# Dilated attention items with joined visits: two PSUM banks taken in turn by transpositions and value products, in place of one bank for each

## The chip, the cores and the metric

The kernel runs on one core of one Trainium2 chip, in one launch. The metric is the device time of that launch in microseconds (us). A core has five engines that follow their own instruction streams and meet through semaphores: TensorE (PE: matrix products and transpositions; the loading of its weights is shown as PEld), VectorE (DVE), ScalarE (ACT), GpSimd (POOL) and SyncE (SP), which here issues the DMAs. Matrix products land in PSUM, which has eight banks of 128 partitions by 512 floats; ACT and DVE read them from there.

## What is computed

One layer of an encoder block on x (1 x 1024 x 1024, float32) with three attention branches. The change lies in the first, the dilated window attention, of 24 heads of 64 in three groups of eight (window and dilation 128/1, 512/4, 2048/16). Cut to its core, the reference does this for one group:

```python
# positions regrouped by residue class mod dilation; then a band of blocks
sc = jnp.einsum('znqhd,znkhd->znhqk', qb, kw).astype(jnp.float32) * (dh ** -0.5)
sc = jnp.where(valid[None, :, None], sc, NEG_INF)
m = jnp.max(sc, axis=-1, keepdims=True)
p = jnp.exp(sc - m)
l = jnp.sum(p, axis=-1, keepdims=True)
o = jnp.einsum('znhqk,znkhd->znqhd', (p / l).astype(v.dtype), vw)
lse = (m + jnp.log(l))[..., 0]
```

The three groups' outputs are then weighted by a softmax over their `lse`, gated, projected, and merged with the other two branches (grouped-query attention; cross-attention into a memory of 256), followed by an output projection and a norm.

## The kernel before

The kernel goes through stages: norm and projections of the memory branch, the grouped-query branch, the dilated items (here about 600 to 1135 us), the merge, the output projection. In every stage but the last, PE's own order is written out by hand in the code. The two interleaved streams are:

- **Dense units.** A unit is one 128-column slice of the input projection: two halves of 24 products each (`dense`, lines 143, 145, 147: two-part weights `wh`, `wl` by two-part activations `hh`, `hl`) into a bank `d`, of which there are two, taken in turn. After each half, DVE reads `d` (rotary product into `t1a`, `t2a`, lines 830 and 831; or the values, line 862), and POOL adds the rotary parts.
- **Pieces of the dilated items.** An item is one pair of heads in one of the three groups, so there are twelve. `plan` writes out its pieces in a fixed order, over eight query tiles T:
  - `scores` (line 918): query by key into banks `s1`, four tiles at a time, at the end of the item before and at T = 3.
  - `soft` (lines 930 to 938): DVE adds the mask and takes the row minimum of the negated scores; ACT takes exponentials into `pra`, two or four instructions per tile.
  - `trans` (lines 955, 964): PE transposes the probabilities of a tile into a `tr` bank, in two to four blocks, and ACT copies it to `app` (line 967). It runs two tiles behind `soft`, so those of tiles 6 and 7 fall into the next item.
  - `values` (line 895): value blocks are transposed into `tr` at T = 4, 5, 6, and copied by ACT to `avs` (line 897).
  - `pv` (line 981): value products of four tiles into a bank `ov`, and ACT copies it to `og` (line 989). The first four tiles come at T = 7, the other four at T = 3 of the next item. Each is joined into one visit with the `scores` of other tiles, which follow it directly on PE.
  - `stats` (line 1000): the row statistics are transposed into `tr` and copied by ACT to `sr` (lines 1003 to 1007), once for each item, at T = 2 of the next.

`weave` lets the two streams take turns on PE by costs that are given in the code (216 for a dense product, 109 for a transposed block, and so on). The other engines' instructions follow from these through a scheduler with priorities.

Banks come from small helpers. `phase_psum` opens the pool of a stage with the number of banks of each kind; `pss1` hands out the next `s1` bank, `pst` the next `tr` bank (128 x 4 x 128), `pso` the next `ov` bank (128 x 512). With one bank of a kind, a new tile's first write waits until the reader of the last tile is done; with two, it waits for the reader of the tile before that one. Six banks are given out to the stage's pool, two go to `d`.

Of the kernel before, what the change touches and what calls it, by code (L numbers as in the profile page):

```python
# [50 lines left out]
def block(ctx: ExitStack, tc: tile.TileContext, x, xT, memT, cst, msk, bcst, tabA, gpost,  # L51
# [15 lines left out]
    def phase_psum(name, s2=0, s1=0, t=0, o=0):  # L67
        assert 2 * s2 + s1 + t + o <= 6
        bank["n"] = (s2, s1, t, o)
        bank["pool"] = tc.tile_pool(name=name, bufs=1, space=bass.MemoryType.PSUM, reuse_waits="tile")  # L70
        bank["p"] = bank["pool"].__enter__()

    def end_psum():
        bank["pool"].__exit__(None, None, None)
# [4 lines left out]
    def pss1():  # L79
        return bank["p"].tile([P, 512], F32, name="s1", tag="s1", bufs=bank["n"][1])  # L80

    def pst():
        return bank["p"].tile([P, 4, 128], F32, name="tr", tag="t", bufs=bank["n"][2])

    def pso():
        return bank["p"].tile([P, 512], F32, name="ov", tag="o", bufs=bank["n"][3])
# [356 lines left out]
    for k in range(8):  # L443
        if k % 2 == 0:
            load_wkv(k // 2)
        for e in range(2 if k == 0 else 1):
            t = slice(e * 512, e * 512 + 512) if k == 0 else slice(0, S)
# [29 lines left out]
    for c in range(2):  # L477
        t = st.tile([P, 4, 256], F32, name=f"mt{c}", tag=f"xk{c}")
# [311 lines left out]
    close(qp)  # L790
    close(kvp)
    end_psum()
    phase_psum("ps_a", s1=4, t=1, o=1)
    pss1()


# [1 line left out]
    with tc.tile_pool(name="aa", bufs=1, reuse_waits="tile") as aa:  # L798
# [75 lines left out]
        def item(p_, g):  # L874
# [95 lines left out]
            def pv(b):  # L970
                if b == 0:
                    d["og"] = OG[p_, g] = cb.tile([P, S], F32, name="og", bufs=4)
                og, vs = d["og"], d["vs"]
                ov = pso()
                for j in range(4):
                    terms = st.pop(4 * b + j)
                    n = len(terms[0])
                    for i in range(n):
                        for h in range(2):
                            x, z, pp = terms[h][i]  # L980
                            PE.matmul(ov[h * 64:h * 64 + 64, j * 128:j * 128 + 128], vs[:, x, z], pp,  # L981
                                      start=i == 0, stop=i == n - 1)
                if g == 0:
                    dst, src = og[:, b * 512:b * 512 + 512], ov
                else:
                    r = DIL[g] // 2
                    dst = og.rearrange("p (u r) -> p r u", r=DIL[g])[:, b * r:b * r + r]
                    src = ov.rearrange("p (r u) -> p r u", r=r)
                A.activation(dst, src, AF.Copy)

            def stats():
# [35 lines left out]
                soft=[(lambda T=T: soft(T), 300.0) for T in range(NT)],  # L1027
                trans=[(lambda T=T: trans(T), 109.0 * {128: 2, 192: 3, 256: 4}[size[T]]) for T in range(NT)],
                pv=[(lambda b=b: pv(b), 250.0 + sum(213.0 * len(blocks_of(T)) for T in range(4 * b, 4 * b + 4))) for b in range(2)],
                stats=(stats, 109.0))  # L1030

# [118 lines left out]
    with tc.tile_pool(name="mg", bufs=1, reuse_waits="tile") as mg:  # L1150
# [102 lines left out]
        for k in range(8):  # L1253
            raw = wp.tile([P, 1024], F32, name="wr", bufs=WR)
            nc.sync.dma_start(raw, wout[k])
            a = hp.tile([P, D], R, name=f"woh{k}", tag="big")
            b = hp.tile([P, D], R, name=f"wol{k}", tag="big")
            split(a, b, raw)
            wo.append((a, b))
        for T in range(NT):  # L1260
            t = slice(T * 128, T * 128 + 128)
# [166 lines left out]
```

## Time and profile before

| | us |
|---|---|
| runs (three) | 1513.45, 1517.66, 1513.59; median 1513.59 |
| profiled execution, own time | 1517.45 |
| profiled execution, span from first to last instruction | 1515.7 |
| granted TensorE clock over the span (1 is full) | 0.995 |
| dilated items, from the first scores to the last value products | about 602 to 1132 |

The profile is one execution. Rows of the timeline give the start, the length, the engine, the line of the kernel, the operation, output and inputs by the program's names, and the idle time before it with what ended it. A matmul's row is longer than its distance to the next one, since matmuls are pipelined and the profiler models their ends. A row with x3 stands for three such instructions in a run. A line of waits reads: engine, output and line that waited, what it waited for, total us, times, longest.

### The profile page before, as it was taken

Reading aid. Unit: us, or ns where it says so; the run is one execution under the profiler, and the core shown is the slowest. Engines: PE = TensorE matmul, PEld = TensorE weight load, DVE = VectorE, ACT = ScalarE, POOL = GpSimd, SP = SyncE. Lnnn points to the kernel's source line nnn. Section 1 sums busy time; section 2 is a strip of 40 time slices with the busy share of each in tenths; the row PEclk is TensorE's granted clock in tenths of the full one; section 3 lists DMA queues with packets and bytes.
Section 4 is the critical chain, followed back from the end, with each engine's and each line's share of the span. In section 5 each row is a group of like instructions: output and inputs, shape, how many; then the busy total and the mean of one; then the engine's idle time right before and its main releaser. Section 6 shows DMA issues by size and latency. Waiting matters only on the chain.

```text
span 1515.7 us, 20621 instructions
## 1 busy us (share of the span) xinstructions
PE 1479.0 (98%) x7844; PEld 1185.4 (78%) x7844; DVE 838.9 (55%) x1514; ACT 578.3 (38%) x1307; POOL 443.8 (29%) x357
## 2 busy tenths in 40 slices
PE   7999989999999999999999999999999999999998
PEld 7899977666776668888777787877777888888787
DVE  7755567566555426655566567556525432525843
ACT  6533444445444431444434444443443112212321
POOL 1426314444444443321232233123200000223322
PEclk9999999999999999999999999999999999999999
DMA  6332011111121122110221131112126541623432
GB/s 236 104 98 71 29 58 51 63 55 43 60 63 56 42 71 90 42 29 29 62 67 43 43 85 36 38 45 71 56 86 189 171 113 42 209 66 116 127 109 98
DMA packets 55042, 119.77 MB, mean 79 GB/s; under 512 B 13792, under 2 KB 23712, under 8 KB 54816
## 3 DMA queue, kind: packets, MB, share of 16 engines
q1 hardware_dynamic: 54800, 118.34, 24.8%
q8 instruction: 61, 1.00, 0.3%
q14 instruction: 37, 0.30, 0.1%
q10 hardware_dynamic: 144, 0.13, 0.0%
HBM read 96.06 MB, written 22.38 MB: 78 GB/s over the span
## 4 chain that ended last, share of the span: by engine, by line
PE 84%; DVE 7%; ACT 3%; issue 2%; DMA 2%; POOL 1%; SPq 0%; POOLq 0%; DVEq 0%; ACTq 0%
PE d L143 14%; PE d L147 14%; PE d L145 14%; PE sc L125 7%; PE ov L720 4%; PE sc L1282 4%; PE sc L147 3%; PE sc L145 3%; PE sc L143 3%; PE ov L981 2%; PE s L705 2%; PE s L918 2%; PE s L704 2%; PE tr L686 2%; PE d L533 2%
## 5 line engine op out<-in xcount | busy, mean ns | idle before, releaser
L143 PE MATMUL d<-hh,wh 128*128 128x512 f32 x992 | 396.0, 399 | 1.7 <-DVE fth L222 1.7
L147 PE MATMUL d<-hh,wl 128*128 128x512 f32 x992 | 397.4, 401 | 0.0
L145 PE MATMUL d<-hl,wh 128*128 128x512 f32 x992 | 393.4, 397 | 0.0
L105 ACT ACTIVATE wh<-wr 128x1024 fp32r<-128x1024 f32 (+1 forms) x100 | 95.4, 955 | 353.2 <-PE d L145 162.5
L143 PEld LDWEIGHTS d<-hh,wh 128*128 128x128 f32 x992 | 187.2, 189 | 44.9 <-issue 5.0
L145 PEld LDWEIGHTS d<-hl,wh 128*128 128x128 f32 x992 | 187.0, 188 | 42.8 <-issue 5.7
L147 PEld LDWEIGHTS d<-hh,wl 128*128 128x128 f32 x992 | 186.9, 188 | 41.6 <-issue 4.7
L711 POOL TENSOR_TENSOR bl<-bl,bp 128x512 f32<-128x512 f32 x96 | 128.8, 1341 | 141.9 <-ACT bp L707 137.3
L106 DVE TENSOR_TENSOR wl<-wr,wh 128x1024 fp32r<-128x1024 f32 (+1 forms) x100 | 113.9, 1139 | 24.3 <-ACT wh L105 24.1
L687 DVE TENSOR_REDUCE bn<-tr 128x1 f32<-128x512 f32 x128 | 87.6, 689 | 63.6 <-PE tr L686 62.3
L707 ACT ACTIVATE bp<-s 128x512 f32<-128x512 f32 x128 | 75.3, 595 | 84.7 <-PE s L705 84.4
L837 POOL TENSOR_TENSOR aq<-t1a,t2a 128x512 f32<-128x512 f32 x24 | 54.6, 2276 | 173.6 <-DVE t1a L831 167.4
L1183 POOL TENSOR_TENSOR acc<-acc,th 128x1024 f32<-128x1024 f32 x16 | 44.6, 2793 | 204.1 <-DVE th L1182 204.1
L831 DVE SCALAR_TENSOR_TENSOR t2a<-d,tab 32x512 f32<-32x512 f32 x96 | 66.0, 687 | 69.1 <-PE d L147 63.7
L147 PE MATMUL sc<-hh,wl 128*128 128x512 f32 x224 | 87.9, 392 | 2.4 <-DVE wl L106 2.4
L837 POOL TENSOR_TENSOR ak<-t1a,t2a 128x512 f32<-128x512 f32 x24 | 54.6, 2276 | 119.9 <-DVE t1a L830 119.9
L145 PE MATMUL sc<-hl,wh 128*128 128x512 f32 x224 | 87.9, 392 | 0.0
L143 PE MATMUL sc<-hh,wh 128*128 128x512 f32 x224 | 87.9, 392 | 0.0
L830 DVE TENSOR_TENSOR t2a<-d,tab 32x512 f32<-32x512 f32 x96 | 66.0, 687 | 25.1 <-PE d L147 23.9
L930 DVE CUSTOM_DVE_ANT_0 pra<-s,mask 128x192 f32<-128x192 f32 (+2 forms) x192 | 56.8, 349 | 36.2 <-PE s L918 24.4
L967 ACT ACTIVATE app<-tr 128x384 f32<-128x384 f32 (+2 forms) x96 | 45.9, 478 | 80.5 <-PE tr L964 46.3
L125 PE MATMUL sc<-gh,wh 128*128 128x512 f32 x192 | 74.7, 389 | 0.0
(263 smaller groups left out, 2745.7 us busy)
## 6 DMA issues: line engine op xcount, KB each, us to landing
wr<-in_wu SPq DMA_DIRECT2D x76, 512.0 KB
g2d<-fth SPq DMA_DIRECT2D x24, 256.0 KB
wgt<-wgd SPq DMA_DIRECT2D x24, 256.0 KB
ot<-od SPq DMA_DIRECT2D x12, 512.0 KB
gt<-g2d SPq DMA_DIRECT2D x12, 512.0 KB
wr<-in_wbr SPq DMA_DIRECT2D x24, 256.0 KB
thd<-fth SPq DMA_DIRECT2D x20, 256.0 KB
th<-thd SPq DMA_DIRECT2D x10, 512.0 KB
```

The source lines that it names most:

```text
L105: A.activation(dst_h, src, AF.Copy)
L106: V.tensor_tensor(dst_l, src, dst_h.bitcast(F32), op=OP.subtract)
L125: PE.matmul(out_ps, a, b, start=i == 0, stop=i == n - 1)
L143: PE.matmul(dst, wh[:, k, :], hh[k][:, t], start=k == 0, stop=False)
L145: PE.matmul(dst, wh[:, k, :], hl[k][:, t], start=False, stop=False)
L147: PE.matmul(dst, wl[:, k, :], hh[k][:, t], start=False, stop=k == 7)
L687: V.tensor_reduce(st[i]["n"][:, j, c:c + 1], s, axis=AX.X, op=OP.min)
L707: A.activation(pp, s, AF.Exp, scale=-1.0)
L711: G.tensor_tensor(lsum[i % 2], lsum[i % 2], pp, op=OP.add)
L830: return V.tensor_tensor(out, x, y, op=OP.mult)
L831: return V.scalar_tensor_tensor(out, x, scale, y, op0=OP.mult, op1=OP.mult)
L837: G.tensor_tensor(half_of(o, half, g), classes(t1, g), classes(t2, g), op=OP.add)
```

## The change

In the dilated stage the pool has two banks of the kind `tr` and none of the kind `ov`; the value products of `pv` take the next `tr` bank, seen as 128 x 512. The number of banks in the pool stays six. So all visits that write these banks (`trans`, `values`, `stats`, `pv`) take the two in turn, in the order of the program.

```diff
@@ -790,7 +790,7 @@
     close(qp)
     close(kvp)
     end_psum()
-    phase_psum("ps_a", s1=4, t=1, o=1)
+    phase_psum("ps_a", s1=4, t=2)
     pss1()
@@ -971,7 +971,7 @@
                 if b == 0:
                     d["og"] = OG[p_, g] = cb.tile([P, S], F32, name="og", bufs=4)
                 og, vs = d["og"], d["vs"]
-                ov = pso()
+                ov = pst().rearrange("p a b -> p (a b)")
                 for j in range(4):
                     terms = st.pop(4 * b + j)
                     n = len(terms[0])
```

## The prediction

> **What bounds the kernel now.** I read the page first (busy time), then the busy times by stage, then who TensorE (PE) waited for in the stretch that the change touches, then that stretch in order of time.
>
> ```profile
> span 1515.7 us, 20621 instructions
> ...
> PE 1479.0 (98%) x7844; PEld 1185.4 (78%) x7844; DVE 838.9 (55%) x1514; ACT 578.3 (38%) x1307; POOL 443.8 (29%) x357
> ```
>
> PE has work for nearly the whole span, and no other engine passes 55%. So time can come only from gaps on PE. The dilated items run from about 600 to 1135 us; their busy time by stretches (first the length, then each engine's busy time, the granted clock behind the engines) is:
>
> ```profile
> core 0: us, PE busy (x) PEld busy (x) DVE busy (x) ACT busy (x) POOL busy (x), PEclk, DMA share, GB/s
> 600.00:1135.00 535.00, 525.28 (x3163) 422.06 (x3162) 308.73 (x724) 225.07 (x673) 134.59 (x79) 1.00 0.18 52
> ...
> 775.00:820.00 45.00, 42.05 (x255) 33.56 (x255) 29.80 (x56) 17.63 (x57) 14.64 (x6) 1.00 0.12 39
> 820.00:865.00 45.00, 45.00 (x279) 36.44 (x276) 24.89 (x71) 19.07 (x58) 8.89 (x8) 1.00 0.15 41
> ```
>
> PE is idle for 9.7 us of this stage, and unevenly: 2.95 us in one stretch of 45 us, nothing in the next. The view of waits, for PE in this stage, names every one of these gaps:
>
> ```profile
> PE tr L955 <- ACT avs L897: 4.8, 6, 0.8
> PE tr L955 <- ACT app L967: 2.3, 3, 0.8
> PE tr L1000 <- ACT app L967: 1.8, 3, 0.6
> PE tr L964 <- ACT app L967: 0.7, 3, 0.2
> ```
>
> Fifteen waits, 9.6 us, all of one kind: a transposition into `tr` waits until ScalarE (ACT) has copied the visit before it out of the only `tr` bank. The value products write `ov`, the other bank, and are in no line. The groups by line say the same: the two kinds of probability transpositions and the statistics carry the idle time (last column).
>
> ```profile
> L964 PE MATMUL tr<-cs,pra 128*128 128x128 f32 x160 | 26.9, 274 | 0.8 <-ACT app L967 0.7
> L955 PE MATMUL tr<-cs,pra 128*128 128x128 f32 x120 | 20.2, 277 | 7.1 <-ACT avs L897 4.8 <-ACT app L967 2.3
> ...
> L1000 PE MATMUL tr<-cs,sts 128*32 128x128 f32 x12 | 3.3, 278 | 1.8 <-ACT app L967 1.8
> ```
>
> **What one stall really costs.** Two places show the pattern; it recurs in each of the later three head pairs. First, the seam between two items; PE and ACT rows in order of time (start, length):
>
> ```profile
> 772.11 0.60 ACT L989 ACTIVATE og<-ov 128x512 f32<-128x512 f32 x1 [1.03 <-PE ov L981]
> ...
> 776.82 0.39 PE L143 MATMUL d<-hh,wh 128*128 128x512 f32 x1
> 777.04 0.40 PE L145 MATMUL d<-hl,wh 128*128 128x512 f32 x1
> 777.57 0.57 ACT L967 ACTIVATE app<-tr 128x512 f32<-128x512 f32 x1
> 778.19 0.55 PE L955 MATMUL tr<-cs,pra 128*128 128x128 f32 x3 [0.75 <-ACT app L967]
> 779.27 0.39 PE L147 MATMUL d<-hh,wl 128*128 128x512 f32 x1
> 779.74 0.47 ACT L967 ACTIVATE app<-tr 128x384 f32<-128x384 f32 x1
> 780.26 0.28 PE L1000 MATMUL tr<-cs,sts 128*32 128x128 f32 x1 [0.60 <-ACT app L967]
> ...
> 781.53 0.39 PE L147 MATMUL d<-hh,wl 128*128 128x512 f32 x1
> 781.77 0.49 PE L955 MATMUL tr<-cs,pra 128*128 128x128 f32 x3
> ```
>
> Unhindered, a dense product starts 0.22 to 0.23 us after the one before (776.82, 777.04), although its row is 0.39 to 0.40 long, since the rows overlap. So a stall is start to start less 0.23: 778.19 - 777.04 - 0.23 = 0.92, where the idle column says 0.75. Each reported gap is really 0.17 longer: 9.6 + 15 x 0.17 = 12.1 us. Stalls of less than 0.17 us are hidden in the overlap altogether or show as no idle time; at 1127.06 below one costs 1127.06 - 1126.65 - 0.23 = 0.18. I count eight such in the stage's timeline, about 1.1 us together. In all PE loses 13.2 us here.
>
> **The change, part by part.** *The order.* As built, every engine has the same instructions in the same order as before. `weave` steers by costs that are not edited, and the ACT copies keep their places. Only waits differ on PE: the first value product of each of 24 visits gets a wait for ACT, and one transposition more has one. No DMA and no queue moves.
>
> *One bank to two for transpositions.* 140 transposition visits and 24 value-product visits now share two banks in turn, so a visit waits for the copy two visits back, not one. At 778.19 that is the value product, copied out at 772.11 + 0.60 = 772.71; PE could have started at 777.27. The whole 0.92 goes. The probabilities that it reads were made an item earlier. The statistics at 780.26 then come 0.92 earlier with their own 0.76 gone (start 778.58) and need the copy that ends at 777.57 + 0.57 = 778.14: free. The transposition at 781.77 would now come 1.68 earlier, at 780.09, and needs the copy that ends at 779.74 + 0.47 = 780.21. If that copy doesn't move (ACT works in order), PE waits 0.12 us for it, and 0.05 us more for the signal (780.21 to 780.26 above): 0.17 us, three times over, so 0.5 us given back. The second place lies inside an item, where value transpositions (copied by L897) alternate with probability transpositions:
>
> ```profile
> 799.63 0.57 ACT L897 ACTIVATE avs<-tr 128x512 f32<-128x512 f32 x1
> 800.26 0.55 PE L955 MATMUL tr<-cs,pra 128*128 128x128 f32 x3 [0.81 <-ACT avs L897]
> 800.84 0.49 ACT L967 ACTIVATE app<-tr 128x384 f32<-128x384 f32 x1 [0.64 <-PE tr L955]
> ...
> 804.42 0.57 ACT L897 ACTIVATE avs<-tr 128x512 f32<-128x512 f32 x1
> 805.04 0.55 PE L955 MATMUL tr<-cs,pra 128*128 128x128 f32 x3 [0.79 <-ACT avs L897]
> ...
> 807.28 0.60 PE L895 MATMUL tr<-cs,vda 128*128 128x128 f32 x4
> ```
>
> Each of the two L955 rows stalls for 0.81 + 0.17 = 0.98 and 0.79 + 0.17 = 0.96. The second needs, two visits back, the copy of 800.84 to 801.33, and PE comes to it at 805.04 - 0.98 - 0.96 = 803.10: free. The value transposition at 807.28 comes 1.94 earlier, at 805.34, and needs the copy that ends at 804.99: free with 0.35 to spare, even if ACT gains nothing.
>
> *The value products' new wait.* Queued behind it on PE are the dense products and the scores of the next block; ACT's copy L989 waits for it. Before, `ov` was free for a whole half item; now the bank is that of the transposition two visits back. The tightest places are at the end of the stage, where the visits crowd:
>
> ```profile
> 1125.57 1.06 ACT L989 ACTIVATE og<-ov 128x512 f32<-128x512 f32 x1
> 1126.65 0.40 PE L143 MATMUL d<-hh,wh 128*128 128x512 f32 x1
> 1127.06 0.44 PE L964 MATMUL tr<-cs,pra 128*128 128x128 f32 x2
> 1127.53 0.39 ACT L967 ACTIVATE app<-tr 128x256 f32<-128x256 f32 x1 [0.53 <-PE tr L964]
> 1131.44 0.77 PE L981 MATMUL ov<-app,avs 128*64 128x128 f32 x10
> ```
>
> The value products at 1131.44 need the copy that ends at 1127.53 + 0.39 = 1127.92: 3.5 us early. The reverse, a transposition that needs a value product's copy, is tightest at 1127.06: PE is there at 1126.88, the copy ended at 1126.63. So the new waits are met before PE comes to them. A wait that is already met shows no price where transpositions carry one now (the one at 781.77 starts 0.24 us after the row of 781.53, as a dense product would), so I take 0 for the 25 new ones. A wait can't gain time, so their bounds are 0 and 25 times the 0.01 us that the view resolves.
>
> *What is late next.* The two `d` banks. With 1.94 us gained by 805.04, the dense product of this row pair would start at 804.19 and needs VectorE's last read of its bank, which ends at 804.03:
>
> ```profile
> 803.34 0.69 DVE L830 TENSOR_TENSOR t1a<-d,tab 128x512 f32<-128x512 f32 x1
> 806.13 0.39 PE L143 MATMUL d<-hh,wh 128*128 128x512 f32 x1
> ```
>
> 0.16 us are left there, in one place of each of three items: it holds narrowly, and each 0.1 us that VectorE slips costs 0.3 us in all.
>
> **The sum.** 13.2 - 0.5 = 12.7 us. What follows the stage starts from PE's last products in it and moves up with them. The profiled execution (span 1515.7, own time 1517.45) becomes 1503.0 and 1504.8. It lies 3.9 above the median of the three runs (1513.59; the others 1513.45 and 1517.66), and no view shows where those 3.9 us are; I take the stage's stalls to be the same in all. **1513.6 - 12.7 = 1500.9 us.** About 0.3% (4.5 us) is what a measurement of this kernel can tell from no change.
>
> **The rivals.** *1. The waits come back one visit later.* If ACT's copies are the real pace (they sit in its queue behind exponentials that wait for VectorE), the second stall of each pair stays: the one at 805.04 (0.96) and that of the statistics (0.76), three times each, 5.2 us; the gain is 7.5, the time 1506.1. For it: the copies at 777.57 and 799.63 come late after their transpositions. Against: the spare times worked out above, 0.35 us and more.
>
> *2. The gain is lost at the next stage.* PE's longest wait behind the items is this:
>
> ```profile
> 1173.64 0.50 PE L147 MATMUL sc<-hh,wl 128*128 128x512 f32 x1 [2.35 <-DVE wl L106]
> ```
>
> If what feeds it is tied to transfers that don't move, it grows by 12.7 us and the time stays 1513.6. Against: the chain of waits leads from it back to the last filler and value products of the items, which move. That the change doesn't remove the bank as the cause of the waits at all would give the same time; but all four wait lines name a copy out of `tr`.
>
> *3. Slower: the granted clock.* After the wait of 1173.64 the clock is low for a while:
>
> ```profile
> 1174.00:1178.00 4.00, 4.00 (x12) 3.16 (x11) 3.35 (x3) 0.00 (x0) 1.21 (x1) 0.57 0.42 131
> ```
>
> That episode costs 4 x (1 - 0.57) = 1.7 us. If taking the banks in turn brought such an episode at each of the 24 value-product visits, it would cost 41 us: 1513.6 - 12.7 + 41 = 1542. It eats the gain from 8 episodes and is slower by 0.3% from 11. Against: the stage runs at 1.00 throughout, with gaps of 0.8 us and `d` banks that already take turns; the change shortens gaps. The Trainium skill, page "TensorE: Matmul & The Clock Gate", section "A second HAM failure mode: psum-queue depth-cycling", tells of a kernel that cycled through PSUM banks each iteration and whose PE idled between groups often enough for its clock to swing. No row of this stage agrees with it: the clock there is 1.00.
>
> **How the numbers follow.** Forecast 0.76; rival 1 0.13; rival 2, or a bank that isn't the cause, 0.06; rival 3 0.05. The first two are faster than 1509.1: 0.89; within 0.3%: 0.06; slower: 0.05. The low end is all 13.2 us and no slow episode at 1174 (1.7): 1498.7. The high end takes in rival 1 with a little more, 1507.0; it also covers the forecast in a run like the slowest of before (1500.9 + 4.1).
>
> **What would show it.** Right: in the profile after, PE's waits in the items keep no line of `tr` for a copy beyond some 0.2 us in three places; the value products have no idle time; the stretch like 775 to 820 is as full as the next; the last value products come at about 1118.7 instead of 1131.44; VectorE's and ACT's busy time are unchanged. Wrong: lines L955 or L1000 with waits of 0.6 us and more (rival 1), a wait at L147 near 1160 of over 10 us (rival 2), a clock under 1.00 between 600 and 1120 us (rival 3), or a new line of `d` waiting for VectorE (the narrow place).

## The result, and the profile after

The changed kernel took 1502.62 us (median of six, 1501.67 to 1505.91), the kernel before 1514.92 us in the six runs beside it (1513.45 to 1517.66). The ratio is 0.9921, 95% interval 0.9907 to 0.9936: 0.8% faster, 12.3 us. In a later comparison it was 0.9906 (0.989 to 0.9922). The forecast was 1500.9 us and 12.7 us.

The page after, its first part:

```profile
span 1500.2 us, 20621 instructions
...
PE 1474.2 (98%) x7844; PEld 1185.7 (79%) x7844; DVE 838.9 (56%) x1514; ACT 576.4 (38%) x1307; POOL 444.7 (30%) x357
```

The instructions are as many as before and the other engines' busy time is the same within 2 us. The share of PE is the same 98%, so the page alone doesn't tell that something was mended; the busy times of the stage do. A row of them gives the stretch and its length, then busy time and number of instructions of PE, PEld, DVE, ACT and POOL, then the granted clock, the DMA share and GB/s. From the first scores to the last value products, before:

```profile
602.47:1131.44 528.97, 519.25 (x3126) 417.32 (x3125) 304.86 (x716) 223.17 (x670) 133.83 (x79) 1.00 0.18 52
```

and after:

```profile
602.33:1118.46 516.13, 515.78 (x3125) 418.85 (x3124) 305.49 (x716) 221.13 (x670) 134.25 (x79) 1.00 0.18 53
```

The stage is 12.84 us shorter (528.97 to 516.13), with PE idle for 0.35 us in place of 9.7. PE, DVE, ACT and POOL run the same instructions in the same order as before. The view of PE's waits has no line left in this stretch. The groups by line, after (last column: idle time before them):

```profile
L981 PE MATMUL tr<-app,avs 128*64 128x128 f32 x640 | 40.2, 276 | 0.0
...
L964 PE MATMUL tr<-cs,pra 128*128 128x128 f32 x160 | 26.6, 272 | 0.0
L955 PE MATMUL tr<-cs,pra 128*128 128x128 f32 x120 | 19.8, 273 | 0.3
```

L955 had 7.1 us, L964 0.8. The value products, which have the new wait, still show none. The second place of the prediction, in order of time after (rows of PE, its weight load PEld, ACT and DVE):

```profile
798.11 0.60 PE L895 MATMUL tr<-cs,vda 128*128 128x128 f32 x4
...
800.25 0.69 DVE L830 TENSOR_TENSOR t1a<-d,tab 128x512 f32<-128x512 f32 x1
800.73 0.40 PE L147 MATMUL d<-hh,wl 128*128 128x512 f32 x1
801.00 0.19 PEld L143 LDWEIGHTS d<-hh,wh 128*128 128x128 f32 x1 [0.31 <-DVE t1a L830]
801.00 0.50 PE L143 MATMUL d<-hh,wh 128*128 128x512 f32 x1
801.33 0.58 ACT L897 ACTIVATE avs<-tr 128x512 f32<-128x512 f32 x1
801.34 0.39 PE L145 MATMUL d<-hl,wh 128*128 128x512 f32 x1
802.26 0.60 PE L895 MATMUL tr<-cs,vda 128*128 128x128 f32 x4
```

ACT's copy at 801.33 is that of the transpositions at 798.11 and still starts 2.6 us after their end (798.71); but PE needs it only at 802.26, and it ends at 801.91. The copy has not become quicker, PE has stopped waiting for it.

The profiles differ by 15.5 us of span, more than the runs' 12.3. Behind the items the wait at L147 is 1.69 us where it was 2.35, and the clock didn't fall after it. The row and the window behind it:

```profile
1160.00 0.50 PE L147 MATMUL sc<-hh,wl 128*128 128x512 f32 x1 [1.69 <-DVE wl L106]
```

```profile
1160.00:1164.00 4.00, 4.00 (x17) 3.30 (x18) 3.15 (x3) 0.00 (x0) 0.96 (x1) 1.00 0.42 131
```

Before, the clock behind this wait (1174 to 1178) stood at 0.57, which cost 1.7 us. These 2.4 us of the two profiles' difference (0.66 and 1.7) vary between executions, as the experiments show; the length of the stage after came out the same when it was profiled again (516.12 us).

### The profile page after: what moved, and what is told of

Its sections match the earlier page's. It is cut to its first block, busy times and chain, and to the rows that moved or that the text cites. A ratio compares the mean times of both kernels' runs of the same rounds, so it can differ in the third digit from the quotient of the medians.

```text
span 1500.2 us, 20621 instructions
## 1 busy us (share of the span) xinstructions
PE 1474.2 (98%) x7844; PEld 1185.7 (79%) x7844; DVE 838.9 (56%) x1514; ACT 576.4 (38%) x1307; POOL 444.7 (30%) x357
## 4 chain that ended last, share of the span: by engine, by line
PE 88%; DVE 5%; DMA 2%; ACT 2%; issue 2%; POOL 1%; SPq 0%; POOLq 0%; DVEq 0%; ACTq 0%
PE d L143 14%; PE d L147 14%; PE d L145 14%; PE sc L125 7%; PE ov L720 4%; PE sc L1282 4%; PE sc L147 3%; PE sc L143 3%; PE sc L145 3%; PE tr L981 3%; PE s L918 2%; PE s L705 2%; PE s L704 2%; PE tr L686 2%; PE d L533 2%
## 5 line engine op out<-in xcount | busy, mean ns | idle before, releaser
L143 PE MATMUL d<-hh,wh 128*128 128x512 f32 x992 | 396.4, 400 | 1.8 <-DVE fth L222 1.8
L147 PE MATMUL d<-hh,wl 128*128 128x512 f32 x992 | 397.4, 401 | 0.0
L143 PEld LDWEIGHTS d<-hh,wh 128*128 128x128 f32 x992 | 187.1, 189 | 47.1 <-issue 5.0
L147 PEld LDWEIGHTS d<-hh,wl 128*128 128x128 f32 x992 | 187.0, 188 | 42.1 <-issue 4.7
L147 PE MATMUL sc<-hh,wl 128*128 128x512 f32 x224 | 87.3, 390 | 1.7 <-DVE wl L106 1.7
L143 PE MATMUL sc<-hh,wh 128*128 128x512 f32 x224 | 87.3, 390 | 0.0
L125 PE MATMUL sc<-gl,wh 128*128 128x512 f32 x192 | 74.7, 389 | 0.0
```

What stands on the lines that cost most here:

```text
L125: PE.matmul(out_ps, a, b, start=i == 0, stop=i == n - 1)
L143: PE.matmul(dst, wh[:, k, :], hh[k][:, t], start=k == 0, stop=False)
L147: PE.matmul(dst, wl[:, k, :], hh[k][:, t], start=False, stop=k == 7)
```

## The experiments

Times are compared with the kernel before on the same chip: 1516.2 us (1512.6 to 1519.16) for the first four, 1517.45 us (1514.07 to 1519.2) for the last two.

### One bank for all: is it the sharing or the second bank?

```diff
-    phase_psum("ps_a", s1=4, t=2)
+    phase_psum("ps_a", s1=4, t=1)
```

> The changed kernel with one tr bank instead of two, so that transpositions and value products share a single bank and the sixth bank of the pool lies idle. My theory (what counts is that a visit waits for the copy two visits back, not that the value products moved): all the waits of before return, 13.1 us as before plus at most some 0.5 us where a transposition now waits for a value product's copy at the end of the stage; 1515 us (1513 to 1518), and the PE waits on tr are again L955, L1000 and L964 with about 9.6 us together, none of them at L981. Rival (the gain came from the value products sharing the bank, or from the changed placement of the program): the time stays at 1502 to 1504.

Measured: 1516.04 us, ratio 1.0004 (0.9994 to 1.0014). PE's waits around this stage:

```profile
PE tr L955 <- ACT avs L897: 4.8, 6, 0.8
PE sc L147 <- DVE wl L106: 2.4, 1, 2.4
PE tr L955 <- ACT app L967: 2.3, 3, 0.8
PE tr L1000 <- ACT app L967: 1.8, 3, 0.6
PE tr L964 <- ACT app L967: 0.7, 3, 0.2
PE tr L964 <- ACT og L989: 0.3, 1, 0.3
```

All four lines of before are back with the same sums. Only one is new, 0.3 us for a value product's copy, at the crowded end. The stage:

```profile
602.00:1131.43 529.43, 519.42 (x3125) 417.19 (x3124) 304.87 (x716) 223.22 (x670) 133.79 (x79) 1.00 0.17 52
```

So seven banks do nearly what eight did before: `ov` as a bank of its own was worth 0.46 us of the stage (529.43 less 528.97; the idle column shows 0.3 of it), and the same bank as a second `tr` is worth 13.30 us (529.43 less 516.13). The Trainium skill, page "Perfetto Trace Analysis", section "Matmul Optimizations", advises to use all eight banks. Here that alone isn't enough: the kernel before used eight and was as slow as this one with seven.

### Two `tr` banks and an `ov` bank, with one score bank less

```diff
-    phase_psum("ps_a", s1=4, t=1, o=1)
+    phase_psum("ps_a", s1=3, t=2, o=1)
```

> The kernel of before with two tr banks and one ov bank, taken from the scores, which get three banks instead of four. My theory: the waits on tr go as in the change, but each of the 24 score visits writes four banks at once, and the fourth now waits until VectorE has read the first for two tiles: in the trace of before, the third of those reads ends some 1.9 us after the visit's start, while PE would be there after 0.75 us, so some 1.1 us each, 27 us in all; 1502.6 + 27 = 1530 us (1520 to 1545), with L918 as a new line of PE's waits. Rival (any two banks for the transpositions do, whoever gives one up): 1502 to 1504, and no line L918.

Measured: 1527.58 us, ratio 1.008 (1.0065 to 1.0096). The waits on `tr` are gone here too. The group of the scores, the first visit, and the part of the second one that waited longest:

```profile
L918 PE MATMUL s<-ak,aq 64*128 64x192 f32 (+2 forms) x384 | 51.8, 349 | 12.7 <-DVE sts L930 12.7
```

```profile
602.70 1.45 PE L918 MATMUL s<-ak,aq 64*128 64x192 f32 x10
604.52 1.13 PE L918 MATMUL s<-ak,aq 64*128 64x256 f32 x6 [0.37 <-DVE sts L930]
605.58 0.50 PE L147 MATMUL d<-hh,wl 128*128 128x512 f32 x1
...
618.90 1.86 PE L918 MATMUL s<-ak,aq 64*128 64x256 f32 x6 [1.63 <-DVE sts L930]
```

The first visit takes 605.58 - 602.70 = 2.88 us; before, such a visit took 1.82. Over the 24 visits I add up 62.8 us against 35.3: 27.5 us, of which the idle column shows 12.7. The wait of 1.63 us was also followed by a stretch of low clock, in which its visit took 4.97 us:

```profile
620.00:630.00 10.00, 10.00 (x40) 7.84 (x39) 4.18 (x12) 4.09 (x15) 0.00 (x0) 0.71 0.07 26
```

The kernel gains the 13 us and pays twice that. The low clock is in the profiled run (1529.63 us at a mean clock of 0.994); the three others took 1527.40 to 1527.73 us at 0.997. Where the bank comes from decides.

### The copies twice, with one bank and with two

In each of the two kernels, the copies of probabilities and of values out of `tr` are done twice in a row:

```diff
                 A.activation(vs[:, i0:i0 + n].rearrange("p b h d -> p b (h d)"), tp[:, :n], AF.Copy)
+                A.activation(vs[:, i0:i0 + n].rearrange("p b h d -> p b (h d)"), tp[:, :n], AF.Copy)
...
                 A.activation(pp[:, :k], tp[:, :k], AF.Copy)
+                A.activation(pp[:, :k], tp[:, :k], AF.Copy)
```

> The kernel of before, with ScalarE's copy out of tr after each probability and value transposition done twice in a row (the same result, 128 copies more, about 0.45 us each). My theory: with one bank the copy's length is on PE's path; moving every copy's end back by 0.45 us in the rows of before raises the sum of stalls from 13.1 to 26.3 us, over 37 places instead of 24: 1515 + 13 = 1528 us (1522 to 1536). Rival (ScalarE's pace sets the stage whichever the number of banks): the same rise here and in the changed kernel with the copies doubled. If copies are not on the path at all: 1515.

> The changed kernel with the same doubled copies. My theory: with two banks the copies have 1.2 us or more to spare at nearly all places, so only the three places that keep a wait grow (0.27 to 0.7 us) and the one at the end of the stage by 0.2 us: 1502.6 + 1.5 = 1504 us (1503 to 1508). Rival (ScalarE's pace sets the stage): it rises as much as the kernel of before does, to about 1516.

Measured: before with doubled copies 1535.78 us, ratio 1.0132 (1.0115 to 1.0149); changed with doubled copies 1505.48 us, ratio 0.993 (0.9915 to 0.9945). Stage lengths: 546.63 and 518.21 us, so the same edit costs 17.7 us with one bank and 2.1 us with two. ACT's work rose by some 60 us in both:

```profile
602.80:1149.43 546.63, 524.92 (x3125) 414.78 (x3124) 304.63 (x716) 283.08 (x798) 133.48 (x79) 1.00 0.17 50
```

```profile
601.48:1119.69 518.21, 516.68 (x3125) 418.41 (x3124) 305.56 (x716) 279.99 (x798) 133.96 (x79) 1.00 0.18 53
```

(The fourth busy time is ACT's.) With one bank, L956, the old L955, waits for both kinds of copy (its lines are one or two higher through the edit), and the other transpositions show another 8.5 us of idle time:

```profile
PE tr L956 <- ACT avs L898: 7.2, 7, 1.4
PE tr L956 <- ACT app L969: 6.0, 4, 1.7
```

with two, all that the view of waits names in the items is

```profile
PE tr L1002 <- ACT app L969: 1.2, 3, 0.4
```

ACT's pace is therefore not the bound; the length of a copy is on PE's path with one bank and off it with two. This rules out the first rival. My 13 us for the one-bank kernel were too small: I moved each copy's end back by one copy's length, but ACT works in order, and a doubled copy also holds up those behind it. That this is where the missing 4.5 us lie I have argued, not shown.

### The statistics after the first transposition, and the change again

```diff
-                if T == 2 and pre:
-                    out += [(lambda: None, 300.0), pre["stats"]]
...
                 elif it:
                     out.append(it["trans"][T - 2])
+                if T == 2 and pre:
+                    out.append(pre["stats"])
```

> The changed kernel with the statistics of the item before transposed after the first probability transposition of the new item instead of before it (and without the empty 300-cost piece ahead of them), so that this transposition needs a copy made one visit earlier. My theory: the three short waits that the change leaves (0.27 us each at the seams after the first group's items) go, the dilated stage gets 0.8 us shorter (516.1 to 515.3 us from the first scores to the last value products), and the time falls by no more than that, 1501.8 us, which the measurement can't tell from the changed kernel. Rival (ScalarE's queue is late at the seam whatever the visit): the waits move to the statistics or to the next transposition and the stage stays at 516 us or grows.

> The changed kernel as it is, on the same chip as the run with the statistics moved, for a comparison with it: 0.992 of the kernel before. The stage of the dilated items takes 516.1 us again (my theory: it is set by waits that don't vary between executions), while the clock after the wait at the start of the next stage may or may not fall (1.5 us), which would explain a part of the spread between executions; rival: the spread lies in the items, and the stage's length differs by a microsecond or more.

Measured: with the statistics moved 1500.43 us (1499.31 to 1500.84), ratio 0.9891 (0.9876 to 0.9907); the change again 1501.99 us (1500.92 to 1505.13), ratio 0.9906 (0.989 to 0.9922). For the items the rival was right. The waits move to the statistics,

```profile
PE tr L1000 <- ACT app L967: 1.1, 3, 0.4
```

and the stage takes 516.20 us against 516.12 in the change run again. ACT's queue is late at this seam whichever visit asks. The 1.6 us between the medians are not in the stage. In the profiles most of the difference lies behind it: from the last value products to the end it is 379.6 us here, 381.7 and 382.7 in the two profiles of the changed kernel, and the wait of PE at L147 is missing from this kernel's waits. On DVE the product of weights and outputs (L1117), which stands ahead of what PE needs there, waited 4.96 us for a transfer in the changed kernel,

```profile
1154.32 2.02 DVE L1117 TENSOR_TENSOR og<-og,wgt 128x1024 f32<-128x1024 f32 x1 [4.96 <-DMA wgt<-wgd]
```

and hardly here:

```profile
1149.47 2.03 DVE L1117 TENSOR_TENSOR og<-og,wgt 128x1024 f32<-128x1024 f32 x1 [0.19 <-DMA wgt<-wgd]
```

The wait has in part moved: the product of L1117 before this one waited 2.96 us here and not at all in the changed kernel. As built, loads of `wgt` stand earlier in SP's order here. I haven't separated that from the rest of the edit, so what shortened the part behind the items is open. The two kernels' runs don't overlap, but 0.1% is less than what I said a measurement can tell, so I claim only that this version is no slower.

The change again gave the same stage, 516.12 us, and a longer wait at L147, 2.85 us, after which the clock stayed full:

```profile
1162.00:1166.00 4.00, 4.00 (x19) 3.27 (x19) 3.10 (x3) 0.00 (x0) 0.90 (x1) 1.00 0.41 131
```

## Why the prediction was right

- **The cause.** All of the stage's waits were for the single `tr` bank. The shared single bank brings them back to the tenth, the second bank removes them. Shown.
- **The size of a stall.** Start to start less 0.23 us gave 13.2 us less 0.5 left over, 12.7; the stage shrank by 12.84. The idle column alone (9.6 us) would have said three quarters of it. That the two agree to 0.14 us is partly luck. Set side by side row by row, the two profiles hold the same 3126 PE products of this stage, and the 23 counted stalls come out at 13.1 us. But a stalled visit of several blocks also loses 0.06 us between its first two blocks (such rows are 0.55 long in place of 0.49): 16 visits, 0.9 us, which the sum lacks, and 0.2 us lie in differences too small to count. Against these stand 1.0 us left at the seams, where the sum has 0.5, and 0.45 us at the `d` banks, where it has nothing: 13.1 + 0.9 + 0.2 - 1.0 - 0.45 = 12.8.
- **What stays.** I put 0.17 us at three seams for the copy that doesn't move. The copy and the rows around it, after:

```profile
778.07 0.47 ACT L967 ACTIVATE app<-tr 128x384 f32<-128x384 f32 x1
778.09 0.39 PE L147 MATMUL d<-hh,wl 128*128 128x512 f32 x1
778.59 0.55 PE L955 MATMUL tr<-cs,pra 128*128 128x128 f32 x3
778.90 0.47 PE L143 MATMUL d<-hh,wh 128*128 128x512 f32 x1
...
780.60 0.49 PE L955 MATMUL tr<-cs,pra 128*128 128x128 f32 x3
780.84 0.48 PE L145 MATMUL d<-hl,wh 128*128 128x512 f32 x1
```

  778.59 - 778.09 - 0.23 = 0.27 us, 0.05 us after the copy's end at 778.54: the place and the reason are right, the size was 0.10 us short. The stalled visit also holds PE for 0.31 us (to 778.90) where the unhindered one at 780.60 holds it for 0.24. Both together, three times, make 1.0 us in place of 0.5.
- **Spare time.** I worked out 0.35 us for the value transposition inside the item. After, it comes at 802.26 and its bank is free at 801.91: 0.35.
- **What is late next.** The `d` bank was to hold with 0.16 us. It did not. DVE's read ends at 800.25 + 0.69 = 800.94, PE's product starts at 801.00, 0.27 us after the one before, and the next one at 801.34, 0.34 us after it, each instead of 0.23: 0.15 us lost, in three items 0.45. The idle column of PE shows nothing of it, but the weight load at 801.00 waits for DVE's read, so the prediction's last sign of being wrong, a wait of `d` for VectorE, came true at a small price. A change that speeds up PE further here will meet DVE.
- **The value products' wait.** No idle time at L981. Right.
- **What follows.** The last value products come at 1118.46 (1118.7 forecast), and the wait at L147 moved up with them, against the second rival.
- **The clock.** The stage runs at 1.00. The page "TensorE: Matmul & The Clock Gate" of the Trainium skill, section "A second HAM failure mode: psum-queue depth-cycling", speaks of a swinging clock where banks are cycled and PE idles between groups; taking two banks in turn brought none. The one episode in the items, in the kernel with three score banks, came behind a wait of PE of 1.63 us; that the turns of the banks caused it isn't shown.
- **The absolute time** was forecast 1.7 us too low, of which 1.3 is that the kernel before had a median of 1513.59 in three runs and 1514.92 in six.

## What to carry to other kernels

When the busiest engine waits in many short, equal gaps, ask which buffer has one copy and whose reader is late; then look for a buffer that is never waited for and let both uses take the two in turn, as long as the order on every engine stays the same. A gap's cost is read from start to start, not from the idle column, which here left out a quarter. Before taking the buffer from another user, work out how much of its present depth that user needs: the scores needed all four banks, the value products none of their own.

## What the hardware showed that I had not expected

The length of a wait doesn't settle what the clock does after it, at least for the lengths seen here. After the wait at L147 in the merge it fell to 0.57 over 4 us in the profile of before (wait of 2.35 us) and in the changed kernel with doubled copies (2.6 us), and it fell in the kernel before with doubled copies too (2.6 us; 0.83 over the 10 us from 1190). It stayed at 1.00 in the changed kernel (1.69 us), in the kernel with one shared bank and in the change run again (2.85 us):

```profile
1174.00:1178.00 4.00, 4.00 (x19) 3.32 (x18) 3.15 (x3) 0.00 (x0) 0.96 (x1) 1.00 0.42 131
```

This is the kernel with one shared bank, after a wait of 2.4 us, in the very window in which the kernel before stood at 0.57. Two executions of one and the same kernel differ as well. Near 53 us, far from the change, PE waits 1.76 us at L143 in both profiles of the changed kernel; in the first the clock stays full, in the second it falls:

```profile
30.00:60.00 30.00, 27.40 (x141) 22.55 (x141) 21.54 (x47) 14.68 (x31) 18.92 (x28) 1.00 0.26 80
```

```profile
30.00:60.00 30.00, 28.10 (x135) 23.18 (x136) 21.02 (x46) 13.41 (x29) 18.95 (x28) 0.94 0.25 80
```

The Trainium skill, page "TensorE: Matmul & The Clock Gate", section "What's actually happening", says that the clock is set by a window that runs freely, so that the same kernel differs from run to run; these waits agree. An episode is worth 1.7 us, so one profile's span can mislead by that much: here the two spans overstate the gain.

This also bears on the 3.9 us between the profiled run of before and its median, which the prediction could not place. Of the 13 runs of the kernel before beside the first four experiments, the four with a mean clock of 0.997 or 0.998 took 1512.6 to 1515.05 us, the six with 0.995, the profiled run's value, 1516.2 to 1519.16. So the clock goes with a part of the spread. It isn't all of it: the ten runs with one shared bank have 0.996 or 0.997 throughout and spread over 5.4 us.
